# One set of three chain buffers, earlier loads of B11, and transposes spread among products, in a hybrid block on one core

## The chip, the core and the metric

The kernel runs on one core of one Trainium2 chip. The metric is device time in microseconds (us) of one execution. Engines: TensorE (PE; PEld is its weight load), VectorE (DVE), ScalarE (ACT), GpSimd (POOL) and SyncE (SP), which only issues loads here.

## The reference

A decoder block over 256 tokens of width 2048, all in float32: an mLSTM branch (4 heads of 256) and an attention branch (8 heads of 128), merged by sigmoid gates, a residual, and a squared-ReLU MLP of width 8192.

```python
    for l in range(DEPTH):
        xn = rmsnorm(x, norm_mix_pre[l])
        proj = jnp.einsum('bsd,dc->bsc', xn, w_in[l])
        mq, mk, mv, mo, mi, mf, aq, ak, av, g_m, g_a = split_cols(proj)
...
        h_m = (h * jax.nn.sigmoid(mo.astype(jnp.float32))).astype(dt)
...
        y_m = jnp.einsum('bsc,cd->bsd', h_m, w_branch_m[l])
        y_a = jnp.einsum('bsc,cd->bsd', h_a, w_branch_a[l])
        merged = jax.nn.sigmoid(g_m) * y_m + jax.nn.sigmoid(g_a) * y_a
        mix_out = jnp.einsum('bsd,de->bse', merged, w_out[l])
        x = x + rmsnorm(mix_out, norm_mix_post[l])

        hn = rmsnorm(x, norm_ffn_pre[l])
        u = jnp.square(jax.nn.relu(jnp.einsum('bsd,df->bsf', hn, w_up[l])))
        y = jnp.einsum('bsf,fd->bsd', u, w_down[l])
        x = x + rmsnorm(y, norm_ffn_post[l])
    return x
```

## The kernel before

Every weight comes from HBM once, in units of 1 MB (128 x 2048), and is split for TensorE into two parts: ScalarE casts the high half (`whi`, L175), VectorE subtracts it from the weight (`wlo`, L176). A product of two split operands is three matmuls (high by high, high by low, low by high), in `mm_tok` (L199), `mm_feat` (L194), `mm_feat_one` (L221) and `mm_factor` (L232, L236, L238). `whi` and `wlo` have four buffers each, two units.

The work is a list of steps; a step is a triple: load and split of its unit, its products, and what follows them (`post`). The loop at the end walks the list and emits the load and split of step i ahead of the products of step i-1. SP issues the loads in that order, and a load waits there until its buffer is free. Within that, a scheduler orders each engine's instructions.

The stages in order: projections (attention, mLSTM and output gate mo); gates and branches; the output product and the residual; the MLP.

**Gates.** The merge gates g_m and g_a are 4 column groups c. In group 0 the plain products are taken: `gate_steps(0, "m")` and `gate_steps(0, "a")`. Groups 1 to 3 go by `seven_steps(c)`: the two gates by two halves of the tokens make a 2 x 2 block product that seven products (p1, p2, p6, q3, q4, q5, q7) compute instead of eight, from sums of weight blocks. Each product has two steps u (two units of rows). Their left operands are x's (`xw`) and four prepared sums `fac`, which `open_gates` makes (ScalarE L678, VectorE L679) from tiles x that lie in `k8`. The weight sums build up in buffers: t starts as block B11 (a plain load on SP, L714, in `w_p1`), GpSimd adds a block to it by an accumulating load (L716) for q5, VectorE adds more for p6 and q4. z is a plain load (L706) and an accumulating load (L707) for q7. t lies in `k8`, a set of two buffers of 1 MB; z has a buffer of its own. `mixed` deals other steps among the seven: gates of group 0, then the branch products (`branch_steps`), whose `evac` multiplies by the gates. After group 3, `merged` transposes the sums (L797) and splits them into `mg` (L803).

**Residual.** `last_mix` computes the last column quarter of the output product for both halves h of the tokens; `residual(h)` makes the norm, adds to x in four pieces e (L886), transposes each (L891) and splits it into `hw`, pair by pair (ScalarE L896, VectorE L897). `hw` is the moving operand of the MLP's up products (L221 to L223). The splits of the first two up units are kept in places of their own (`first_places`).

**MLP.** Eight chunks of the width. For each but the last, `group(j, p)` takes the down product by the same seven-product scheme: `b12` (L1037) is loaded into `k8`, `bt` = B11 + b12 (L1038) is in `k8`, later + b22 (L1044), + b21 (L1060); b22 and b21 lie in `rawl`, two buffers. GpSimd accumulates into b12 (L1053). The operands `xs` come from `factors` (L970, L980 to L993) on ScalarE and VectorE. Up products of the next chunk (U) stand between the down steps (D).

Of the kernel before, what the change touches and what calls it, by code (L numbers as in the profile page):

```python
# [82 lines left out]
def tile_hybrid_block(ctx, tc, xT, xtok, pos, pre, small, wmix, wa, wi, wg, wbr, wo, wu, wd,  # L83
# [17 lines left out]
    def k8(name):  # L101
        return pk.tile([P, 2048], F32, name=name, tag="k8", bufs=2)
# [96 lines left out]
    def mm_tok(accs, parts, mov, kbase, start, stop, halves=(0, 1), n=512):  # L199

        for k, h in [(k, h) for k in range(4) for h in halves]:
# [489 lines left out]
    def gate_steps(c, n):  # L691

        for u in range(4):
            tok_step(wg["ma".index(n), c, u], ("g", n, c), xmov, u,
                     lambda h, acc: tanh(gate(n, c)[:, h], acc, h), bank=sm_tile)

    def seven_steps(c):
# [6 lines left out]
        def load_z(u):  # L704
            r["z", u] = pool["f"].tile([P, 2048], F32, name="z", tag="z", bufs=1)
# [81 lines left out]
    def merged(c):  # L787

        m = mg[c] = pool["f"].tile([P, 4, 2, T], F32R, name="mg", tag="fac", bufs=4)
        src = gt.pop(("m", c))  # L790
        del gt["a", c]
        for q in range(2):
            ps = sm_tile()
            for j in range(2):
                for h in range(2):
                    b = 2 * j + h
                    PE.transpose(out=ps[:, b * P:(b + 1) * P],  # L797
# [528 lines left out]
```

## Time and profile before

| | |
|---|---|
| median of 3 runs | 1507.71 us (1507.64 to 1510.67) |
| profiled execution | 1508.53 us, span 1506.7 us |
| TensorE busy | 1428.2 us (95%) |
| VectorE busy | 1182.1 us (78%) |
| ScalarE busy | 829.1 us (55%) |
| mean granted clock of TensorE | 0.975 of 2.4 GHz |
| loads | 297.28 MB, mean 197 GB/s |
| gates and branches | about 361 to 667 us of the span |
| residual | about 745 to 775 us |
| MLP | about 775 to 1500 us |

A matmul's busy time in the rows overlaps the next one's, so the pitch of products is read from starts. "Idle before" stands in brackets in a timeline, with what ended it.

### The profile page before, as it was taken

What the parts mean: (1) busy time and instruction counts of PE and PEld (TensorE: products, weight loads), DVE (VectorE), ACT (ScalarE), POOL (GpSimd) and SP (SyncE); (2) the same over time, 40 slices, a digit from 0 to 9 for tenths busy, and PEclk for the clock granted to TensorE, in tenths of its full rate; (3) what the DMA queues carried; (4) which work ended last, traced back from release to release, by engine and by line L of the source; (5) the groups of instructions that cost most, each with busy time, mean ns of one, the idle gap of its engine ahead of it and who ended that gap; (6) DMA issues with size and microseconds to landing.
All of it is one profiled execution on the core that took longest, in us unless ns stands there. A gap on an engine that the chain in (4) does not pass through costs nothing.

```text
span 1506.7 us, 20304 instructions
## 1 busy us (share of the span) xinstructions
PE 1428.2 (95%) x7892; PEld 1226.1 (81%) x7892; DVE 1182.1 (78%) x1506; ACT 829.1 (55%) x1132; POOL 24.7 (2%) x38
## 2 busy tenths in 40 slices
PE   8999999998798999999879999999999999999997
PEld 6888888886576877788679898989889798998985
DVE  7787766776576888854556989898999989889895
ACT  8655555555455556634555665555555555555562
POOL 0000000000000000000000000000000000000000
PEclk9999999998899999999989999999999999999999
DMA  7644444443669686655527476566575575665561
GB/s 229 223 166 173 168 168 168 168 168 140 197 189 271 206 285 202 231 220 183 221 84 252 168 236 203 180 222 215 203 242 199 176 250 177 215 226 194 196 223 57
DMA packets 46321, 297.28 MB, mean 197 GB/s; under 512 B 5392, under 2 KB 7568, under 8 KB 11664
## 3 DMA queue, kind: packets, MB, share of 16 engines
q1 hardware_dynamic: 42336, 268.71, 48.5%
q0 software_dynamic: 3744, 27.26, 9.5%
q8 instruction: 62, 1.02, 0.3%
q14 instruction: 35, 0.29, 0.1%
q10 hardware_dynamic: 144, 0.01, 0.0%
HBM read 293.86 MB, written 2.10 MB: 196 GB/s over the span
## 4 chain that ended last, share of the span: by engine, by line
PE 79%; DVE 11%; DMA 5%; ACT 2%; issue 2%; SPq 0%; DVEq 0%; ACTq 0%
PE acc L223 8%; PE acc L221 8%; PE acc L222 8%; PE acc L194 8%; PE acc L238 7%; PE acc L232 7%; PE acc L236 7%; DVE wlo L176 5%; PE acc L211 4%; PE acc L206 4%; PE acc L210 4%; PE acc L195 4%; PE sm L206 2%; PE sm L210 2%; PE sm L211 2%
## 5 line engine op out<-in xcount | busy, mean ns | idle before, releaser
L175 ACT CAST whi<-raw 128x1024 fp32r<-128x1024 f32 (+2 forms) x396 | 399.0, 1014 | 346.9 <-PE acc L222 109.3
L176 DVE TENSOR_TENSOR wlo<-raw,whi 128x1024 fp32r<-128x1024 f32 (+2 forms) x396 | 463.2, 1179 | 149.6 <-ACT whi L175 144.7
L223 PE MATMUL acc<-hw,wlo 128*128 128x256 f32 x992 | 284.5, 287 | 0.1
L222 PE MATMUL acc<-hw,whi 128*128 128x256 f32 x992 | 283.8, 286 | 0.0
L221 PE MATMUL acc<-hw,whi 128*128 128x256 f32 x992 | 283.1, 286 | 0.0
L223 PEld LDWEIGHTS acc<-hw,wlo 128*128 128x128 f32 x992 | 191.7, 193 | 4.3 <-DVE wlo L176 1.2
L221 PEld LDWEIGHTS acc<-hw,whi 128*128 128x128 f32 x992 | 191.0, 193 | 5.1
L222 PEld LDWEIGHTS acc<-hw,whi 128*128 128x128 f32 x992 | 191.1, 193 | 2.1
L232 PE MATMUL acc<-whi,xs 128*128 128x512 f32 x440 | 175.7, 400 | 17.4 <-ACT whi L175 17.4
L194 PE MATMUL acc<-xw,whi 128*128 128x512 f32 x512 | 183.5, 397 | 0.0
L238 PE MATMUL acc<-wlo,xs 128*128 128x512 f32 x440 | 174.0, 399 | 1.5 <-DVE wlo L176 1.2
L236 PE MATMUL acc<-whi,xs 128*128 128x512 f32 x440 | 174.7, 397 | 0.0
L195 PE MATMUL acc<-xw,wlo 128*128 128x256 f32 x512 | 146.5, 286 | 0.0
L175 ACT CAST whi<-bt 128x1024 fp32r<-128x1024 f32 x84 | 86.0, 1046 | 83.2 <-PE acc L222 40.6
L194 PEld LDWEIGHTS acc<-xw,whi 128*128 128x128 f32 x512 | 96.2, 188 | 22.9 <-issue 1.9
L176 DVE TENSOR_TENSOR wlo<-bt,whi 128x1024 fp32r<-128x1024 f32 x84 | 101.2, 1220 | 13.4 <-ACT whi L175 13.3
L232 PEld LDWEIGHTS acc<-whi,xs 128*128 128x128 f32 x440 | 83.2, 189 | 34.8 <-ACT whi L175 20.7
L238 PEld LDWEIGHTS acc<-wlo,xs 128*128 128x128 f32 x440 | 82.7, 188 | 22.1 <-DVE wlo L176 5.4
L236 PEld LDWEIGHTS acc<-whi,xs 128*128 128x128 f32 x440 | 83.3, 189 | 17.5
L195 PEld LDWEIGHTS acc<-xw,wlo 128*128 128x128 f32 x512 | 96.3, 188 | 1.3 <-issue 0.2
L175 ACT CAST whi<-rawl 128x1024 fp32r<-128x1024 f32 x56 | 58.6, 1047 | 47.5 <-PE acc L222 34.6
L176 DVE TENSOR_TENSOR wlo<-t,whi 128x1024 fp32r<-128x1024 f32 x48 | 57.7, 1222 | 33.9 <-ACT whi L175 32.1
(294 smaller groups left out, 2401.4 us busy)
## 6 DMA issues: line engine op xcount, KB each, us to landing
raw<-in_wu_dram SPq DMA_DIRECT2D x64, 1024.0 KB, 5.0
raw<-in_wi_dram SPq DMA_DIRECT2D x48, 1024.0 KB, 4.9
rawl<-in_wd_dram SPq DMA_DIRECT2D x28, 1024.0 KB, 4.9
raw<-in_wd_dram SPq DMA_DIRECT2D x22, 1024.0 KB, 5.8
raw<-in_wg_dram SPq DMA_DIRECT2D x20, 1024.0 KB, 5.1
raw<-in_wbr_dram SPq DMA_DIRECT2D x16, 1024.0 KB, 5.7
raw<-in_wo_dram SPq DMA_DIRECT2D x16, 1024.0 KB, 4.8
b<-in_wd_dram SPq DMA_DIRECT2D x14, 1024.0 KB, 5.3
```

What stands on the lines that cost most here:

```text
L175: S.copy(out=hi[:, s], in_=r)
L176: V.tensor_tensor(out=lo[:, s], in0=r, in1=hi[:, s].bitcast(F32), op=ALU.subtract)
L194: PE.matmul(out=accs[i][:, 0:2 * T], lhsT=hi, rhs=m, start=k == 0, stop=False)
L195: PE.matmul(out=accs[i][:, 0:T], lhsT=lo, rhs=m[:, 0, :], start=False, stop=k == nk - 1)
L206: first = PE.matmul(out=acc, lhsT=m[:, 0, ts], rhs=hi, start=start and k == 0, stop=False)
L210: PE.matmul(out=acc, lhsT=m[:, 1, ts], rhs=hi, start=False, stop=False)
L221: PE.matmul(out=acc, lhsT=hi, rhs=m[:, 0, :], start=k == 0, stop=False)
L222: PE.matmul(out=acc, lhsT=hi, rhs=m[:, 1, :], start=False, stop=False)
L223: PE.matmul(out=acc, lhsT=lo, rhs=m[:, 0, :], start=False, stop=k == KT - 1)
L232: first = PE.matmul(out=acc, lhsT=f[:, k, 0], rhs=hi, start=start and k == 0, stop=False, skip_group_check=more)
L236: PE.matmul(out=acc, lhsT=f[:, k, 1], rhs=hi, start=False, stop=False, skip_group_check=more)
L238: PE.matmul(out=acc, lhsT=f[:, k, 0], rhs=lo, start=False, stop=stop and k == 3, skip_group_check=more)
```

## The change

The set `k8` gets a third buffer, and takes t, z, b12, bt and b22 (before in `rawl`, which keeps one buffer), and both halves of the second up unit. A load of t is emitted by a hook (`before`) ahead of an earlier step: t of group 1 ahead of two steps of gate m(0), those of groups 2 and 3 ahead of p2(0) and p2(1) of the group before. z's first load follows p1(1) instead of p1(0). q5(1) comes right behind q7(0), and q3 accumulates into q5's bank. gate_steps(0, "m") uses the other kind of bank (`acc`), as does one of the two steps of branch m. The transposes of `merged` are spread over steps (`at`). `residual` is cut into `mix_rstd`, `add_mix`, `turn` and `operand`, dealt among the products of `last_mix`; the first two up units are split at earlier steps (`first_unit`). In the MLP v and u have buffers of their own, and all xs but q4's share one set (`g4`).

```diff
     def k8(name):
-        return pk.tile([P, 2048], F32, name=name, tag="k8", bufs=2)
+        return pk.tile([P, 2048], F32, name=name, tag="k8", bufs=3)
...
-    def gate_steps(c, n):
+    def gate_steps(c, n, bank=sm_tile):
...
+    ahead = {}
+    hooks = {}
+    def before(step, f, *args):
...
+        hooks.setdefault(id(step[1]), []).append(lambda: f(*args))
     def seven_steps(c):
...
         def load_z(u):
-            r["z", u] = pool["f"].tile([P, 2048], F32, name="z", tag="z", bufs=1)
+            r["z", u] = k8("z")
             nc.sync.dma_start(out=r["z", u], in_=w(1, 0, u))
             nc.gpsimd.dma_start(out=r["z", u], in_=w(1, 1, u), accum_op=ALU.add)
...
+        def load_t(u):
+            r["t", u] = k8("t")
+            nc.sync.dma_start(out=r["t", u], in_=w(0, 0, u))
         def w_p1(u):
-            t = r["t", u] = k8("t")
-            nc.sync.dma_start(out=t, in_=w(0, 0, u))
-            parts = split(t)
-            nc.gpsimd.dma_start(out=t, in_=w(1, 0, u), accum_op=ALU.add)
-            if u == 0:
+            parts = split(r["t", u])
+            nc.gpsimd.dma_start(out=r["t", u], in_=w(1, 0, u), accum_op=ALU.add)
+            if u == 1:
                 load_z(0)
             return parts
...
-        banks = dict(p1="a", p2="a", q5="e", q7="b", q4="b", p6="f", q3="g")
+        banks = dict(p1="a", p2="a", q5="e", q3="e", q7="b", q4="b", p6="f")
...
             elif name == "q3":
-                V.tensor_tensor(out=ga[:, 0], in0=ga[:, 1], in1=r["v"], op=ALU.subtract)
-                add(ga[:, 0], a)
+                V.tensor_tensor(out=ga[:, 0], in0=a, in1=r["v"], op=ALU.subtract)
...
-            more = name in ("p2", "q4")
+            more = name in ("p2", "q3", "q4")
...
+        ahead[c] = load_t
         return [step(n, u) for n, u in (
-            ("p1", 0), ("p1", 1), ("q5", 0), ("q7", 0), ("p6", 0), ("q3", 0), ("q5", 1),
+            ("p1", 0), ("p1", 1), ("q5", 0), ("q7", 0), ("q5", 1), ("p6", 0), ("q3", 0),
             ("p6", 1), ("q3", 1), ("q7", 1), ("p2", 0), ("q4", 0), ("p2", 1), ("q4", 1))]
...
         src = ha if n == "a" else hm
+        banks = [sm_tile, sm_tile] if n == "a" else [acc_tile, sm_tile]
...
-                     bank=sm_tile)
...
+                     bank=lambda: banks.pop()())
...
+    def merged(c, q):
+        if q == 0:
+            mg[c] = pool["f"].tile([P, 4, 2, T], F32R, name="mg", tag="fac", bufs=4)
+        m, src, ps = mg[c], gt["m", c], sm_tile()
+        for j in range(2):
...
-    gate_steps(0, "m")
+    def at(k, f, *args):
...
+        src, mm, post = steps[k]
+        steps[k] = src, mm, lambda: (post(), f(*args))
+    gate_steps(0, "m", acc_tile)
...
-    for k, f in ((i - 3, lambda: mlstm_out(3, heads.pop(3))), (i - 2, open_gates)):
...
-    both_gates(1, (gate_steps, 0, "a"))
-    both_gates(2, (branch_steps, 0, "a"), (branch_steps, 0, "m"), (branch_steps, 1, "a"))
-    both_gates(3, (branch_steps, 1, "m"), (branch_steps, 2, "a"), (branch_steps, 2, "m"))
-    then(lambda: [merged(c) for c in range(3)])
+    at(i - 3, lambda: mlstm_out(3, heads.pop(3)))
+    at(i - 2, open_gates)
+    groups = {c: seven_steps(c) for c in SGATES}
+    before(steps[i - 3], ahead[1], 0)
+    before(steps[i - 1], ahead[1], 1)
+    for c in (1, 2):
+        before(groups[c][10], ahead[c + 1], 0)
+        before(groups[c][12], ahead[c + 1], 1)
+    mixed(groups[1], (gate_steps, 0, "a"))
+    mixed(groups[2], (branch_steps, 0, "a"), (branch_steps, 0, "m"), (branch_steps, 1, "a"))
+    mixed(groups[3], (branch_steps, 1, "m"), (branch_steps, 2, "a"), (branch_steps, 2, "m"))
+    i = len(steps)
+    for k, c, q in ((9, 0, 0), (8, 0, 1), (5, 1, 0), (4, 1, 1)):
+        at(i - k, merged, c, q)
     branch_steps(3, "a")
     branch_steps(3, "m")
-    then(merged, 3)
+    for k, c, q in ((0, 2, 0), (1, 2, 1), (3, 3, 0), (3, 3, 1)):
+        at(i + k, merged, c, q)
...
-    def residual(h):
...
+    def mix_rstd(h):
...
+        late["r", h] = r
...
+    def add_mix(h, e):
+        x1 = late["x1"][:, h, e * 512:(e + 1) * 512]
+        pin(V.scalar_tensor_tensor(out=x1, in0=late["mix"][e][:, h], scalar=late["r", h], in1=x1,
+                                   op0=ALU.mult, op1=ALU.add))
+    def turn(h, e):
+        ps = late["ps", h, e] = sm_tile()
+        for j in range(4):
+            k = 4 * e + j
+            pin(PE.transpose(out=ps[:, j * P:(j + 1) * P],
+                             in_=late["x1"][:, h, k * P:(k + 1) * P], identity=ident))
...
+    def operand(h, e):
...
+            S.activation(out=hi, in_=p, func=AF.Copy, scale=g)
+            pin(V.scalar_tensor_tensor(out=lo, in0=p, scalar=g, in1=hi.bitcast(F32), op0=ALU.mult,
+                                       op1=ALU.subtract))
...
-                    mm_tok(late["acc"], units[i], mgmov, 8 + 4 * i, False, i == 1, halves=(h,))
+                    mm_tok(late["acc"], units[i], mgmov, 8 + 4 * i, False, i == 1, halves=(h,),
+                           after_k=turns if h and i else None)
                 if h == 0:
-                    residual(0)
+                    mix_rstd(0)
+                    for e in range(4):
+                        add_mix(0, e)
+        def turns(k):
+            if k > 0:
+                turn(0, k - 1)
+                operand(0, k - 1) if k < 3 else None
         def post():
-            keep_warm(8)
-            residual(1)
+            mix_rstd(1)
+            turn(0, 3)
+            keep_warm(12)
+            for e in range(4):
+                add_mix(1, e)
+                if e in (1, 2):
+                    operand(0, e + 1)
+                turn(1, e)
+                operand(1, e)
+            for h in range(2):
+                for e in range(4):
+                    square(late["x1"][:, h, e * 512:(e + 1) * 512], late["ss2"][:, h, e:e + 1])
             open_mlp()
         steps.append(([wo[14], wo[15]], mm, post))
+    def first_unit(i):
+        def place():
+            if i == 0:
+                a = pa.tile([P, 2, 2, 1024], F32R, name="wu0", tag="hm")
+                return [(a[:, h, 0], a[:, h, 1]) for h in range(2)]
+            b = [k8("wu1").bitcast(F32R) for _ in range(2)]
+            return [tuple(t[:, 1024 * h:1024 * h + 1024] for t in b) for h in range(2)]
+        places[len(steps)] = place
+        steps.append(([wu[i]], late.setdefault("first", []).extend, lambda: None))
...
     for e in range(4):
...
+            if (e, u) in ((2, 1), (2, 3)):
+                first_unit(u // 2)
     last_mix()
...
-        late["v"] = g4("v")
+        late["v"] = f.tile([P, 2, 512], F32, name="v")
...
-            uh[c] = g4("u", (4, T))
+            uh[c] = pool["f"].tile([P, 4, T], F32, name="u", tag="u", bufs=2)
...
-        if name[1] in ("p1", "q5", "p6"):
+        if name[1] != "q4":
             f = g4("xs", (4, 2, P)).bitcast(F32R)
         else:
-            f = pool["f"].tile([P, 4, 2, P], F32R, name="xs", tag="xs", bufs=4)
+            f = pool["f"].tile([P, 4, 2, P], F32R, name="xs", tag="xs", bufs=1)
...
-        return pool["f"].tile([P, 2048], F32, name="rawl", tag="rawl", bufs=2)
+        return pool["f"].tile([P, 2048], F32, name="rawl", tag="rawl", bufs=1)
...
         def w_t2():
-            r["22"] = long_raw()
+            r["22"] = k8("b22")
...
-    def first_places():
...
+    first = {}
+    def mm_first(units):
+        first["a"] = [acc_tile(), acc_tile()]
+        mm_feat_one(first["a"], late["first"], hmov, tail=4)
+    steps.append(([], mm_first, lambda: first_up(*first["a"])))
...
             src = steps[i][0]
+            for f in hooks.get(id(steps[i][1]), ()):
+                f()
```

Where rows move. First TensorE's queue at the end of gate m(0) and the start of group 1. Names: `mo`'s last products are L194/L195, gate products L206, L210, L211 (L207, L211, L212 in the new lines), `sm<-qkm` and `sm<-mv,ml_s` are the last mLSTM head's small products, `sm<-ident,t` its transposes. Before:

```order
L195 MATMUL acc<-xw,wlo 128x256
L538 MATMUL sm<-ident,t_3484 128x128 x2
L478 MATMUL sm<-rows,ident 128x384
L538 MATMUL sm<-ident,t_3486 128x128 x2
L488 MATMUL sm<-qkm 128x256 x2
L491 MATMUL sm<-qkm 128x128 x2
L499 MATMUL sm<-mv,ml_s 128x258
L503 MATMUL sm<-mv,ml_s 128x258
L505 MATMUL sm<-mv,ml_s 128x258
L206 MATMUL sm<-whi,xw 128x512
```

And now, at one of the places among the gate products, and, in the second fence, at their end:

```order
L491 MATMUL sm<-qkm 128x256
L494 MATMUL sm<-qkm 128x128 x2
L207 MATMUL acc<-whi,xw 128x512
L211 MATMUL acc<-whi,xw 128x512
L212 MATMUL acc<-wlo,xw 128x512
```

```order
L212 MATMUL acc<-wlo,xw 128x512
L235 MATMUL acc<-whi,xw 128x512
L239 MATMUL acc<-whi,xw 128x512
L241 MATMUL acc<-wlo,xw 128x512
...
L541 MATMUL sm<-ident,t_3679 128x128 x2
L541 MATMUL sm<-ident,t_3681 128x128 x2
L235 MATMUL acc<-whi,xw 128x512
```

The small products stood in a row ahead of the gate products and are now among them; p1(1,0) (L235, L239, L241, 12 products) follows the gate products, and the head's transposes, which lead to `fac`, stand between p1(1,0) and p1(1,1).

SP's queue of loads, from the start of the kernel to group 2. `wa`, `wi`, `wg` and `wbr` are the weights of the attention projections, of the others, of the gates and of the branches; p_i is the positions. Before:

```order
L158 DMA raw<-in_wa_dram 128x1040
L324 DMA p_i<-in_pos_dram 128x256
L158 DMA raw<-in_wa_dram 128x1040 x7
L158 DMA raw<-in_wi_dram 128x2048 x48
L158 DMA raw<-in_wg_dram 128x2048 x7
L706 DMA z<-in_wg_dram 128x2048
L714 DMA t<-in_wg_dram 128x2048 x2
L158 DMA raw<-in_wg_dram 128x2048
L706 DMA z<-in_wg_dram 128x2048
L158 DMA raw<-in_wg_dram 128x2048 x4
L706 DMA z<-in_wg_dram 128x2048
L158 DMA raw<-in_wbr_dram 128x2048
```

And now:

```order
L724 DMA t<-in_wg_dram 128x2048
L327 DMA p_i<-in_pos_dram 128x256
L158 DMA raw<-in_wa_dram 128x1040 x7
L158 DMA raw<-in_wi_dram 128x2048 x48
L158 DMA raw<-in_wg_dram 128x2048 x7
L724 DMA t<-in_wg_dram 128x2048
L716 DMA z<-in_wg_dram 128x2048
L158 DMA raw<-in_wg_dram 128x2048
L716 DMA z<-in_wg_dram 128x2048
L158 DMA raw<-in_wg_dram 128x2048 x4
L724 DMA t<-in_wg_dram 128x2048
L158 DMA raw<-in_wbr_dram 128x2048
```

The first t stands ahead of p_i, the second ahead of z; group 2's first t stands where its z stood, and that z five rows later.

VectorE's queue at the third chunk start of the MLP. Before:

```order
L1079 TENSOR_TENSOR y_6293<-y_6293,acc_9314 128x512
L970 TENSOR_TENSOR xs_9303<-u_9005,xs_9303 128x4x128
L985 TENSOR_TENSOR s_b_9298<-s_a_9293,u_8618 128x512
...
L970 TENSOR_TENSOR xs_9300<-s_b_9298,xs_9300 128x4x128
L1038 TENSOR_TENSOR bt_9409<-raw_9358,b12_9408 128x2048
L176 TENSOR_TENSOR wlo_9387<-raw_9384,whi_9386 128x1024
```

And now:

```order
L1129 TENSOR_TENSOR y_6291<-y_6291,acc_9312 128x512
L1088 TENSOR_TENSOR bt_9407<-raw_9356,b12_9406 128x2048
L1035 TENSOR_TENSOR s_b_9296<-s_a_9291,u_8616 128x512
...
L1020 TENSOR_TENSOR xs_9298<-s_b_9296,xs_9298 128x4x128
L1020 TENSOR_TENSOR xs_9301<-u_9003,xs_9301 128x4x128
```

The sum bt stands nine rows earlier, right behind y, and an operand xs later.

## Rows read from the trace of the kernel before

**Rows 1.** The page: busy times, and the chain that ended last by engine.

```profile
PE 1428.2 (95%) x7892; PEld 1226.1 (81%) x7892; DVE 1182.1 (78%) x1506; ACT 829.1 (55%) x1132; POOL 24.7 (2%) x38
PE 79%; DVE 11%; DMA 5%; ACT 2%; issue 2%; SPq 0%; DVEq 0%; ACTq 0%
```

**Rows 2.** TensorE's waits by releaser: us in total, times, longest.

```profile
PE acc L232 <- ACT whi L175: 29.3, 12, 7.0
PE sm L891 <- DVE x L886: 12.9, 4, 3.9
...
PE sm L797 <- DVE mg L803: 3.2, 1, 3.2
```

**Rows 3.** Window of groups 1 and 2: busy times, clock, DMA share, GB/s.

```profile
403.00:550.00 147.00, 137.35 (x546) 105.98 (x547) 114.70 (x99) 82.33 (x87) 6.81 (x8) 0.95 0.78 232
```

**Rows 4.** Windows at half clock: PE, PEld, DVE, ACT, POOL busy; clock; DMA share; GB/s.

```profile
363.48:373.71 10.23, 5.92 (x15) 4.70 (x16) 3.26 (x10) 1.76 (x4) 0.00 (x0) 0.50 0.24 94
401.02:407.85 6.83, 4.81 (x11) 3.35 (x12) 2.36 (x2) 1.99 (x2) 0.86 (x1) 0.50 1.03 272
482.94:489.77 6.83, 6.31 (x16) 4.86 (x16) 5.20 (x5) 3.46 (x5) 0.84 (x1) 0.50 0.82 146
...
1093.93:1097.35 3.42, 3.04 (x12) 2.85 (x13) 3.42 (x6) 1.41 (x3) 0.84 (x1) 0.50 0.87 271
```

**Rows 5.** The chain in order of time: start, us, what.

```profile
24.41 3.46 DMA raw<-in_wa_dram
...
393.32 4.64 DVE fac L679 x4
397.98 10.61 DMA t<-in_wg_dram
...
409.74 1.24 DVE wlo L176
...
431.51 11.05 DMA raw<-in_wg_dram
...
469.41 11.69 DMA t<-in_wg_dram
```

**Rows 6.** TensorE's timeline at the gates: start, us, instructions, idle before.

```profile
362.62 0.67 PE L488 MATMUL sm<-qkm 128*128 128x256 f32 x2 [1.57 <-DVE ml_e L483]
...
372.25 0.99 PE L206 MATMUL sm<-whi,xw 128*128 128x512 f32 x1
...
391.46 0.38 PE L538 MATMUL sm<-ident,t 128*128 128x128 f32 x2
...
391.92 0.39 PE L210 MATMUL sm<-whi,xw 128*128 128x512 f32 x1
...
395.63 0.40 PE L211 MATMUL sm<-wlo,xw 128*128 128x512 f32 x1
403.00 0.80 PE L232 MATMUL acc<-whi,xw 128*128 128x512 f32 x1 [6.97 <-ACT whi L175]
...
482.30 0.50 PE L232 MATMUL acc<-whi,xw 128*128 128x512 f32 x1 [3.46 <-ACT whi L175]
```

**Rows 7.** DMA issues: count, KB each, median us from issue to landing.

```profile
raw<-in_wu_dram SPq DMA_DIRECT2D x64, 1024.0 KB, 5.0
...
z<-in_wg_dram POOLq DMA_DIRECT2D x6, 1024.0 KB, 11.9
```

**Rows 8.** The chain at the residual's end.

```profile
752.14 0.36 DVE hw L897
...
752.93 0.36 DVE hw L897
...
773.63 1.22 PE acc L221 x4
```

**Rows 9.** MLP: TensorE's waits, 905 to 1450; VectorE's timeline; a window.

```profile
PE acc L232 <- ACT whi L175: 16.9, 7, 2.8
...
1090.82 2.28 DVE L1038 TENSOR_TENSOR bt<-raw,b 128x2048 f32<-128x2048 f32 x1
...
1090.00:1100.00 10.00, 7.17 (x40) 6.17 (x39) 10.00 (x12) 4.17 (x5) 0.84 (x1) 0.83 0.55 142
```

More of the change, by code (lines that the diff above doesn't have):

```diff
@@ L197, in mm_feat, with mm_tok @@
                 after_k(k)
-    def mm_tok(accs, parts, mov, kbase, start, stop, halves=(0, 1), n=512):
+    def mm_tok(accs, parts, mov, kbase, start, stop, halves=(0, 1), n=512,
+               after_k=None):
         for k, h in [(k, h) for k in range(4) for h in halves]:
@@ L211, in mm_tok @@
             PE.matmul(out=acc, lhsT=m[:, 0, ts], rhs=lo, start=False, stop=stop and k == 3)
+            if after_k:
+                after_k(k)
     def mm_feat_one(accs, units, mov, after_k=None, tail=0):
@@ L689, in tanh @@
         S.activation(out=out, in_=src, func=AF.Tanh, scale=rhalf[:, h:h + 1])
-    def gate_steps(c, n):
+    def gate_steps(c, n, bank=sm_tile):
         for u in range(4):
             tok_step(wg["ma".index(n), c, u], ("g", n, c), xmov, u,
-                     lambda h, acc: tanh(gate(n, c)[:, h], acc, h), bank=sm_tile)
+                     lambda h, acc: tanh(gate(n, c)[:, h], acc, h), bank=bank)
+    ahead = {}
+    hooks = {}
+    def before(step, f, *args):
+        hooks.setdefault(id(step[1]), []).append(lambda: f(*args))
     def seven_steps(c):
@@ L784, in branch_steps @@
             tok_step(wbr["am".index(n), c, u], ("b", n, c), lambda k: src[:, k], u, evac, last=1,
-                     bank=sm_tile)
[L787 to L797, printed above, removed]
-                                 in_=src[:, h, (2 * q + j) * P:(2 * q + j + 1) * P],
-                                 identity=ident)
-            hi, lo = (m[:, 2 * q:2 * q + 2, i] for i in range(2))
-            p = ps.rearrange("p (k t) -> p k t", t=T)
-            S.activation(out=hi, in_=p, func=AF.Copy, scale=0.5)
-            V.scalar_tensor_tensor(out=lo, in0=p, scalar=0.5, in1=hi.bitcast(F32), op0=ALU.mult,
-                                   op1=ALU.subtract)
+                     bank=lambda: banks.pop()())
[5 more added lines that the diff above has]
+            for h in range(2):
+                b = 2 * j + h
+                PE.transpose(out=ps[:, b * P:(b + 1) * P],
+                             in_=src[:, h, (2 * q + j) * P:(2 * q + j + 1) * P], identity=ident)
+        hi, lo = (m[:, 2 * q:2 * q + 2, i] for i in range(2))
+        p = ps.rearrange("p (k t) -> p k t", t=T)
+        S.activation(out=hi, in_=p, func=AF.Copy, scale=0.5)
+        V.scalar_tensor_tensor(out=lo, in0=p, scalar=0.5, in1=hi.bitcast(F32), op0=ALU.mult,
+                               op1=ALU.subtract)
     def mixed(first, *parts):
@@ L1182, in down_group @@
         return [(part(n, 0), part(n, 1), part(n, 2)) for n in range(7)]
-    def first_places():
-        a = pa.tile([P, 2, 2, 1024], F32R, name="wu0", tag="hm")
-        b = [k8("wu1").bitcast(F32R),
-             pool["f"].tile([P, 2048], F32, name="wu1", tag="z", bufs=1).bitcast(F32R)]
-        return [[(a[:, h, 0], a[:, h, 1]) for h in range(2)],
-                [tuple(t[:, 1024 * h:1024 * h + 1024] for t in b) for h in range(2)]]
-    feat_step([wu[0], wu[1]], hmov, first_up, tail=4, product=mm_feat_one)
-    places[len(steps) - 1] = first_places
+    first = {}
[3 more added lines that the diff above has]
+    steps.append(([], mm_first, lambda: first_up(*first["a"])))
     for i in range(2, 8):
```

38 lines of the change are left out of this document (7 added, 31 removed).

## The prediction

> **What bounds the kernel now.** The page's busy times come first: TensorE works 95% of the span, VectorE 78%, and the chain that ended last runs through TensorE for 79% [rows 1]. So the end moves only where TensorE waits, or where its products run at half clock after a wait. The waits by releaser say where: casts that feed products of L232 cost 29.3 us in 12 waits, four transposes of the residual 12.9 us, one transpose of merged 3.2 us [rows 2]. The window of gate groups 1 and 2 gives the DMA engines' share, 0.78 [rows 3], so loads there compete. The windows with the granted clock show the second price: after each long wait the clock stands at 0.50, that is 1.2 of 2.4 GHz, for 3.42 to 10.23 us [rows 4]. The chain in order of time names what was late: twice a t load, once a raw load [rows 5]. TensorE's timeline has the waits one by one, and gives a product's pitch: 16 steps from 391.92 to 395.63, so 0.232 us [rows 6]. The own time is 1508.53 us, 1.83 over its span and 0.8 over the median of 1507.71; the sum is made against 1508.53.
>
> **The change part by part.**
>
> *Start of the kernel.* t(1,0) now goes out right behind the first loads, ahead of p_i and seven raw loads. The chain still runs through a load at 24.41 us [rows 5], so a megabyte in front can push what follows by its own length, some 4 us. But the next casts on VectorE don't use what is pushed: they stand ahead of the rotary work that needs p_i. I take 0, bounds -1 and +4.
>
> *The last mLSTM head and gate m(0).* Before, TensorE stops at 361.05, waits 1.57 us, begins the head's last small products at 362.62 and the gate products at 372.25 [rows 6]: 11.2 us, most of them at half clock and with TensorE busy 5.92 of 10.23 us [rows 4], and the first three gate products take 0.8 us more by that clock. Now these products stand among the 96 gate products, which need only raw loads and x. The small ones still cost about 1.2 us (14 of 128 to 384 columns, against 0.232 for 512). The gain is 11.2 + 0.8 - 1.2, some 10.5 us: the last gate product ends at 385.4 instead of 395.9.
>
> *t loads of group 1.* p1(1,0) needs t(1,0), which before was issued behind the third of the fac operations on VectorE (four take 4.64 us from 393.32), so that TensorE waited 6.97 us at 403.00; and p1(1,1) began only when its own t, issued at 397.98, had landed 10.61 us later and ScalarE had cast it, at 409.74, where VectorE's cast begins [rows 5, 6]. Now t(1,0) is there: its 12 products follow the gate ones at once, 2.8 us, to 388.2. t(1,1) is still not early: two of the three k8 slots hold the x tiles that fac reads. The transposes that lead to fac stand behind p1(1,0); before, from these transposes (391.46) to the third fac operation's end it was 5.4 us. So t(1,1) is issued near 393.7. With nothing but z beside it I take 6 us to land (5.0 is a load's median [rows 7], 10.61 the crowded case) and 1.1 for the cast: p1(1,1) starts at 400.8, 9 us before 409.74. The 10.5 us are thus not added to this; much of the idle time moves to a wait of 12 us between p1(1,0) and p1(1,1), with a half-clock stretch behind it as before [rows 4]. Bounds -5 (load of 10.6) and -11.
>
> *The rest of group 1.* A raw load of 11.05 us stands in the chain at 431.51 [rows 5]; with t and z not bunched behind fac it should be shorter. I take -2, bounds 0 and -4.
>
> *Groups 2 and 3.* t(2,0) and t(2,1) are issued ahead of p2(0) and p2(1) of the group before. So the load of 11.69 us at 469.41 goes from the chain, and with it the wait of 3.46 us at 482.30, 0.5 us behind it, and half of the 6.31 us that TensorE was busy at half clock: -7. Group 3 had no such wait at its start. But z now takes the third slot of the same set, which t of the group before holds until q4(1) has been cast: z(2,0) and z(3,0) come later. z needs a plain load and an accumulating load of 11.9 us in the median [rows 7], 18 us with the cast. Ahead of q7(0) stand 36 products of its group and 24 of another step, 14 us, and the slot is freed one step (24 products) before the group's start: 19 to 20 us against 18, and with busy DMA engines 1 us of wait each, +2, bounds 0 and +14 (7 each with the clock).
> The bytes of the stage are the same in less time. At 232 GB/s for 147 us [rows 3] groups 1 and 2 move 34 MB; at 272 GB/s, the most in [rows 4], that is 125 us, so a gain of 17 is not excluded, but loads take longer: +2, bounds 0 and +6.
>
> The Trainium skill, page "DMA: Bandwidth & Descriptors", section "Issuing engines are not separate DMA queues", says that transfers started from any engine run on the same 16 DMA engines and interleave. By that rule an earlier t load is paid for by whatever it runs beside; the trace agrees (10.61 us for t beside another t and z, against a median of 5.0). If all of it were paid at the start, the sum below would be 4 us higher; that is the second of the rivals.
>
> *Turns of merged.* The transposes that stood in one row after group 3 are spread over it, so the wait of 3.2 us for mg [rows 2] goes: -3, bounds 0 and -4. Branch m's second bank (acc) and the q5/q3 bank shared (three VectorE subtractions of 0.7 us fewer, one a group) are off the path: VectorE is busy 114.70 of 147 us there [rows 3]. 0.
>
> *Residual.* h1's 24 products (5.6 us) now cover part of half 0's chain, and its turns stand among them; the four waits were 12.9 us [rows 2]. Against that, VectorE's order puts three casts of the up weights (1.24 us each, as at 409.74 [rows 5]) into the chain for half 0, so a new wait at the first turn is 4 to 5 us. The up products begin near 767.3 instead of 773.63 [rows 8], but then meet operands that are made in pairs (ScalarE, then VectorE), one per 0.79 us from 752.14 to 752.93 [rows 8], 16 for half 1: they give back most of 6.3 us. I take -2.5, bounds -7 and +3.
>
> *MLP, six chunk starts.* The waits for the cast of bt are 16.9 us [rows 9], 2.76 each, and 3.42 us at half clock follow each [rows 4], 1.6 lost: 4.4 each, 26 in all. bt's add (2.28 us) moves nine rows up in VectorE's queue, as b12 has a slot. But VectorE is then busy 10.00 of 10.00 us [rows 9]: what is put ahead of other casts makes these late. Following the products through the new order, stalls of some 0.4 to 1.7 us stand at four or five places ahead of the old one. I take -0.8 each, -5, bounds 0 and -26.
>
> Sum: 0 - 9 - 2 - 7 + 2 + 2 - 3 - 2.5 - 5 = -24.5, so 1508.5 - 24.5 = **1484 us**. In the gate stage -17, in the rest -7.5.
>
> **The rivals.**
> *z becomes the late load.* If the accumulating load runs as slow as t's 10.61 plus 11.9, q7(0) of groups 2 and 3 waits 5 us each and half clock takes 2: +12 instead of +2, 1494. For it: DMA share 0.8; against it: t no longer runs beside it.
> *The first t load is paid at the start.* +4: 1488. For it: the chain runs through loads until 28 us; against it: the casts stand ahead of p_i's work.
> *The change doesn't do what it says:* t(1,1) and z(1,0) land where they did, since fac frees the slots, and everything waits there; the first term falls from -9 to 0: 1493. For it, fac's chain has ScalarE and VectorE steps of other heads ahead; against it, TensorE reaches the transposes some 3 us earlier.
> *The chunk starts are cleared.* VectorE's debt is made good elsewhere, -26 instead of -5: 1463. Against it: 10.00 of 10.
> *Slower.* SP issues in order. z of groups 2 and 3 waits on SP for q4(1)'s slot, and wbr and wg loads stand behind it in the queue. If they land after their products want them, each group pays their landing time. It decides from 12 us a group on (24.5 over two groups); with a load of 10 us behind z's and another behind it, 17 each, 34 in all: 1518. Against it: raw has buffers loaded ahead.
>
> **How the numbers follow.** Forecast 0.48 (own range 1476 to 1491), z late 0.15, start 0.10, no earlier landing 0.10, chunk starts cleared 0.09, slower 0.08. 1465 to 1503 leaves out the slower case and most of the cleared one, 0.17. A measurement of this kernel tells 0.2% (3 us) from no change. Faster takes in all but the slower rival and a tail of the late z: 0.89; same 0.04; slower 0.07.
>
> **What would show it.** Right: gate products follow the mo products with no wait; a wait of 9 to 13 us on L232's successor (L235) at p1(1,1), which begins at 399 to 402; group 2 begins without a wait for t; group 3 begins 15 to 20 us earlier than at 557; small waits at the chunk starts, with new ones ahead. Wrong: waits on casts of z over 3 us, rows of raw that land late behind z, a wait of more than 6 us at turn(0,0), or VectorE with free time at the chunk starts.

## The result, and the profile after

The changed kernel takes 1491.51 us (median of 4 runs, 1489.58 to 1492.45) against 1508.6 us for the kernel before on the same chip: ratio 0.9883, 95% interval 0.9866 to 0.9900. It is 17 us faster where 24.5 were forecast; 1491.5 lies in the range of 1465 to 1503. It also lies just outside the range that the prediction gave to its own mechanism (1476 to 1491), and closer to three rivals (1488, 1493 and 1494) than to 1484, so the time alone does not say which mechanism held; the traces below do.

The page after, to be held against [rows 1], with the DMA queues (packets, MB, share of 16 engines; q1 are SP's loads, q0 GpSimd's):

```profile
PE 1419.9 (95%) x7900; PEld 1216.1 (82%) x7900; DVE 1178.7 (79%) x1503; ACT 830.3 (56%) x1133; POOL 24.7 (2%) x38
...
q1 hardware_dynamic: 42336, 268.71, 48.9%
q0 software_dynamic: 3744, 27.26, 9.7%
```

GpSimd's 27 MB of accumulating loads take 0.36% of the DMA engines' span for each MB, SP's 269 MB 0.18%. That factor of two is not in the prediction, though the page before had it already:

```profile
q1 hardware_dynamic: 42336, 268.71, 48.5%
q0 software_dynamic: 3744, 27.26, 9.5%
```

Most of what the prediction missed hangs on these loads (experiments 3 and 4).

The stages are best compared by the start of the same product in both traces: for the gates by its place in the order, behind them by its number counted from the end. The difference is after minus before, worked out from the two timelines, so from one execution of each kernel:

| product | before | after | difference |
|---|---|---|---|
| first gate m(0) product | 372.25 | 361.16 | -11.1 (of it +1.8 from the start of the kernel) |
| last gate m(0) product | 395.63 | 387.28 | -8.4 |
| p1(1,1) | 409.76 | 402.11 | -7.7 |
| a product near the end of group 1 (p2, q4) | 472.14 | 466.79 | -5.4 |
| third product of group 2's q5 | 494.85 | 480.73 | -14.1 |
| end of group 2 | 554.84 | 544.83 | -10.0 |
| 108 products on, in group 3 | 580.85 | 578.00 | -2.9 |
| first product of the output matrix | 660.75 | 652.75 | -8.0 |
| second up unit of the MLP | 804.65 | 795.43 | -9.2 |
| last product | 1496.98 | 1479.60 | -17.4 |

TensorE's timeline after (start, us, instruction, idle before and what ended it) shows why the gates lose again what they had won:

```profile
361.16 0.39 PE L207 MATMUL acc<-whi,xw 128*128 128x512 f32 x1
...
387.28 0.40 PE L212 MATMUL acc<-wlo,xw 128*128 128x512 f32 x1
...
402.11 0.79 PE L235 MATMUL acc<-whi,xw 128*128 128x512 f32 x1 [11.20 <-ACT whi L175]
...
421.85 0.50 PE L235 MATMUL acc<-whi,fac 128*128 128x512 f32 x1 [4.29 <-ACT whi L175]
...
485.40 0.50 PE L235 MATMUL acc<-whi,fac 128*128 128x512 f32 x1 [2.18 <-ACT whi L175]
...
563.32 0.79 PE L235 MATMUL acc<-whi,fac 128*128 128x512 f32 x1 [4.85 <-ACT whi L175]
```

The first three rows answer to [rows 6] and are as forecast: gate products from 361, a wait of 11.2 us at p1(1,1), which begins at 402.11. The last three are waits that were not there before: for t(1,1) at q5(1) of group 1, for z(2,0) at q7(0) of group 2, and for t(3,0) at q5(0) of group 3. The chain after shows their loads:

```profile
405.61 15.05 DMA t<-in_wg_dram
...
470.70 13.51 DMA z<-in_wg_dram
...
542.01 4.86 DMA z<-in_wg_dram
...
547.46 0.51 POOL z L717
547.96 14.18 DMA t<-in_wg_dram
```

The loads of 15.05, 13.51 and 14.18 us are accumulating ones, issued by GpSimd; the one of 4.86 us is z(3,0)'s plain load, whose end z's accumulating load waits for. GpSimd's timeline shows how they came together; group 3 before:

```profile
534.88 0.84 POOL L707 DMA_DIRECT2D z<-in_wg_dram  x1 [31.46 <-DVE t L710]
557.41 0.86 POOL L716 DMA_DIRECT2D t<-in_wg_dram  x1 [21.69 <-DVE wlo L176]
562.61 0.84 POOL L716 DMA_DIRECT2D t<-in_wg_dram  x1 [4.34 <-DVE wlo L176]
```

and after:

```profile
547.43 0.84 POOL L717 DMA_DIRECT2D z<-in_wg_dram  x1 [52.96 <-DVE wlo L176]
547.96 1.19 POOL L728 DMA_DIRECT2D t<-in_wg_dram  x1
550.27 0.84 POOL L728 DMA_DIRECT2D t<-in_wg_dram  x1 [1.11 <-DVE wlo L176]
```

Before, z's went out 22 us ahead of t's, into its own buffer. Now z waits for the slot that t of the group before leaves (z(3,0)'s plain load goes out at 542.01, before at 529.27, while the group itself begins 10 us earlier), and all three go out within 3 us. They land one after another, 7.78, 14.18 and 17.90 us after their issue, at 555.21, 562.14 and 568.17. In group 2 it is much the same, and in group 1 two of them meet, z(1,0)'s and t(1,1)'s. So z is not the load that got slower, as the medians from issue to landing show, before (z's is 11.9, [rows 7]) and after:

```profile
t<-in_wg_dram POOLq DMA_DIRECT2D x6, 1024.0 KB, 8.6
```

```profile
t<-in_wg_dram POOLq DMA_DIRECT2D x6, 1024.0 KB, 14.6
...
z<-in_wg_dram POOLq DMA_DIRECT2D x6, 1024.0 KB, 7.9
```

Windows over the three late loads (last columns: granted clock, DMA share, GB/s):

```profile
547.96:562.14 14.18, 10.51 (x46) 8.19 (x44) 4.38 (x5) 3.41 (x5) 2.04 (x3) 1.00 0.98 220
470.70:484.20 13.50, 12.52 (x54) 9.80 (x52) 8.66 (x7) 4.88 (x6) 1.70 (x2) 1.00 1.02 227
405.61:420.65 15.04, 11.83 (x50) 8.92 (x48) 8.12 (x6) 4.02 (x5) 1.19 (x2) 1.00 0.95 226
```

The DMA engines are full at 220 to 227 GB/s. The prediction took 272 GB/s as what the stage could still move. That the shared slot brings the loads together is read from these timelines; no run gives z a buffer of its own beside the set of three.

### The profile page after: what moved, and what is told of

It is laid out like the page before. It is cut to its first block, busy times and chain, and to the rows that moved or that the text cites. A ratio compares the mean times of both kernels' runs of the same rounds, so it can differ in the third digit from the quotient of the medians.

```text
span 1489.3 us, 20301 instructions
## 1 busy us (share of the span) xinstructions
PE 1419.9 (95%) x7900; PEld 1216.1 (82%) x7900; DVE 1178.7 (79%) x1503; ACT 830.3 (56%) x1133; POOL 24.7 (2%) x38
## 3 DMA queue, kind: packets, MB, share of 16 engines
q8 instruction: 62, 1.02, 0.3%
## 4 chain that ended last, share of the span: by engine, by line
PE 80%; DVE 10%; DMA 5%; ACT 2%; issue 1%; SPq 0%; POOL 0%; DVEq 0%; ACTq 0%; POOLq 0%
PE acc L194 8%; PE acc L241 8%; PE acc L235 8%; PE acc L239 8%; PE acc L226 7%; PE acc L225 7%; PE acc L224 7%; PE acc L212 5%; PE acc L207 5%; PE acc L211 5%; DVE wlo L176 5%; PE acc L195 4%; DMA t<-in_wg_dram 2%; DMA z<-in_wg_dram 2%; PE sm L207 2%; PE sm L211 2%
## 5 line engine op out<-in xcount | busy, mean ns | idle before, releaser
L226 PE MATMUL acc<-hw,wlo 128*128 128x256 f32 x992 | 280.3, 283 | 1.8 <-DVE wlo L176 1.5
L225 PE MATMUL acc<-hw,whi 128*128 128x256 f32 x992 | 279.4, 282 | 0.0
L224 PE MATMUL acc<-hw,whi 128*128 128x256 f32 x992 | 277.5, 283 | 0.3 <-ACT whi L175 0.3
L226 PEld LDWEIGHTS acc<-hw,wlo 128*128 128x128 f32 x992 | 187.1, 189 | 8.4 <-DVE wlo L176 6.5
L224 PEld LDWEIGHTS acc<-hw,whi 128*128 128x128 f32 x992 | 185.7, 188 | 6.2 <-ACT whi L175 2.7
L225 PEld LDWEIGHTS acc<-hw,whi 128*128 128x128 f32 x992 | 187.0, 188 | 1.6
L241 PE MATMUL acc<-wlo,xs 128*128 128x512 f32 x440 | 174.4, 400 | 10.3 <-DVE wlo L176 10.0
L194 PE MATMUL acc<-xw,whi 128*128 128x512 f32 x512 | 183.6, 397 | 0.0
L235 PE MATMUL acc<-whi,xs 128*128 128x512 f32 x440 | 174.5, 396 | 3.8 <-ACT whi L175 3.1
L239 PE MATMUL acc<-whi,xs 128*128 128x512 f32 x440 | 173.3, 394 | 0.0
L195 PE MATMUL acc<-xw,wlo 128*128 128x256 f32 x512 | 146.4, 286 | 0.0
L194 PEld LDWEIGHTS acc<-xw,whi 128*128 128x128 f32 x512 | 96.2, 188 | 23.1 <-issue 2.1
L241 PEld LDWEIGHTS acc<-wlo,xs 128*128 128x128 f32 x440 | 82.7, 188 | 36.5 <-DVE wlo L176 20.3
L235 PEld LDWEIGHTS acc<-whi,xs 128*128 128x128 f32 x440 | 82.7, 188 | 20.2 <-ACT whi L175 4.9
L207 PE MATMUL acc<-whi,xw 128*128 128x512 f32 (+1 forms) x256 | 95.2, 375 | 2.8 <-ACT whi L175 2.8
L195 PEld LDWEIGHTS acc<-xw,wlo 128*128 128x128 f32 x512 | 96.3, 188 | 1.1
L239 PEld LDWEIGHTS acc<-whi,xs 128*128 128x128 f32 x440 | 82.6, 188 | 17.2
L211 PE MATMUL acc<-whi,xw 128*128 128x512 f32 (+1 forms) x256 | 94.9, 374 | 1.1 <-DVE xw L255 1.1
```

The lines of the kernel that those rows point to most:

```text
L194: PE.matmul(out=accs[i][:, 0:2 * T], lhsT=hi, rhs=m, start=k == 0, stop=False)
L195: PE.matmul(out=accs[i][:, 0:T], lhsT=lo, rhs=m[:, 0, :], start=False, stop=k == nk - 1)
L207: first = PE.matmul(out=acc, lhsT=m[:, 0, ts], rhs=hi, start=start and k == 0, stop=False)
L211: PE.matmul(out=acc, lhsT=m[:, 1, ts], rhs=hi, start=False, stop=False)
L224: PE.matmul(out=acc, lhsT=hi, rhs=m[:, 0, :], start=k == 0, stop=False)
L225: PE.matmul(out=acc, lhsT=hi, rhs=m[:, 1, :], start=False, stop=False)
```

## The experiments

Ratios are to runs of the kernel before beside them on the same chip, with 95% intervals; the changed kernel's is 0.9883 (0.9866 to 0.9900).

**1. t's loads at their written place.**

```diff
-            nc.sync.dma_start(out=r["t", u], in_=w(0, 0, u))
+            tc.keep_in_program_order(nc.sync.dma_start(out=r["t", u], in_=w(0, 0, u)))
```

> The changed kernel, but the six plain loads of t keep their written place in SP's queue, so t(1,0) no longer goes out ahead of p_i at the start. My theory: the early load costs the 1.8 us that the first mLSTM products come later than before, and nothing else hangs on it; so -1 to -2.5 us against the changed kernel, with the last mo product back near 359.4 us instead of 361.2, and p1(1,0) still without a wait behind the gate products. Rival: t(1,0) then lands too late behind the raw loads of gate m(0), p1(1,0) waits 2 us or more, and the gain is used up: within 1 us.

0.9877 (0.9862 to 0.9893). In the trace the first 300 us run 1.2 us earlier than in the changed kernel: in the chain p_i lands after 4.45 us instead of 7.84. p1(1,0) has no wait. The direction is as expected; the gain is too small to show in the ratio. The traces of all these kernels bear it out: the 1861st product of TensorE, near the end of the mo products, starts at 355.76 to 356.42 us in the four traces with t's loads at their written place (experiments 1, 10, 11, 12; 355.87 before the change), and at 356.78 to 358.92 in the nine with the early load.

**2. GpSimd's order t, t, z.**

```diff
-            nc.gpsimd.dma_start(out=r["z", u], in_=w(1, 1, u), accum_op=ALU.add)
+            tc.keep_in_program_order(
+                nc.gpsimd.dma_start(out=r["z", u], in_=w(1, 1, u), accum_op=ALU.add))
...
-            nc.gpsimd.dma_start(out=r["t", u], in_=w(1, 0, u), accum_op=ALU.add)
+            tc.keep_in_program_order(
+                nc.gpsimd.dma_start(out=r["t", u], in_=w(1, 0, u), accum_op=ALU.add))
```

> The changed kernel, but GpSimd issues both accumulating loads of t ahead of those of z in each group, as the code writes them (the scheduler had put z between or ahead). My theory: what groups 1 and 3 wait for (4.29 us at 421.85, 4.85 us at 563.32) is t's accumulating load held behind z's and sharing the DMA engines with it (15.05 and 14.18 us to landing); with t first these take 8 to 10 us, both waits go, and with the half clock behind them -6 to -11 us. Rival: z, which now goes out last, is late for q7(0) instead, and a wait of 3 to 8 us for it takes the place in each group: within 3 us.

0.9969 (0.9953 to 0.9985): 13 us slower than the changed kernel, worse than either expected. Its chain and TensorE's timeline in group 3:

```profile
559.93 18.38 DMA z<-in_wg_dram
...
579.51 0.79 PE L235 MATMUL acc<-whi,fac 128*128 128x512 f32 x1 [9.12 <-ACT whi L175]
```

t's loads land in time, and z, the last to go out, takes 18.38 us in group 3 and is awaited by q7: waits of 4.74, 8.14 and 9.12 us in the three groups. So the order does not make the loads cheaper; it chooses who waits, and how long, by how soon the last one is wanted.

**3. Without z's second block** (q7's right operand is one block instead of a sum of two).

```diff
-            nc.gpsimd.dma_start(out=r["z", u], in_=w(1, 1, u), accum_op=ALU.add)
```

> The changed kernel without z's accumulating loads: q7 then uses one weight block instead of a sum of two, so 6 MB are left out. My theory (accumulating loads in flight together are the late ones): the three waits at 421.85, 485.40 and 563.32 (11.3 us) fall below 1 us each, and with the clock -11 to -17 us. Rival (a slot of the set of three or SP's queue holds t and z up, or the stage's bytes as a whole): the waits stay over 2 us each, and the gain is under 5 us.

0.9779 (0.9761 to 0.9797), 15.7 us less than the changed kernel (the difference of the ratios times 1508.6, here and below). The kernel leaves out 6 MB of loads. TensorE's waits for casts from 400 to 640 us:

```profile
PE acc L235 <- ACT whi L175: 11.2, 1, 11.2
```

Of the waits for ScalarE's casts only the one at p1(1,1) is left, and no wait for VectorE's casts is over 0.74 us. A late slot or SP's queue does not make the waits by itself, since neither is touched by this edit; the 6 MB fewer are not ruled out as the cause until the next experiment.

**4. z's second block by a plain load and VectorE.**

```diff
-            nc.gpsimd.dma_start(out=r["z", u], in_=w(1, 1, u), accum_op=ALU.add)
+            V.tensor_tensor(out=r["z", u], in0=r["z", u], in1=load(w(1, 1, u)), op=ALU.add)
```

> The changed kernel, but z's second block comes by a plain load into one of the three raw buffers and VectorE adds it (2.28 us each, 6 times), in place of GpSimd's accumulating load. My theory: the waits come from accumulating loads lying together, of which two are left, 8 and 13 us; the plain load takes some 5. So the three waits go as without the second block (-15.7 us by the ratios), less what the raw buffers lose: -6 to -14 us. Rival: it is SP's queue and the raw buffers that bound the stage, then the added raw loads make other products wait: no gain, or some us slower.

0.9820 (0.9805 to 0.9835), 9.5 us less. The same bytes come in, so it is the way they come, and not their number, that cost these 9.5 us; the sum takes VectorE 2.29 us each time. Waits of 1.69 and 2.99 us for t(c,0)'s accumulating load are left in groups 2 and 3.

**5. GpSimd's order t, z, t.** load_z(0) stands ahead of t(c,1)'s accumulating load in w_p1, and both are held in that order as in 2.

> The changed kernel with GpSimd's order held at t(c,0), z(c,0), t(c,1) in all three groups, the order in which the products want them; by the trace only group 3's differs (z, t, t). My theory: group 3's wait of 4.85 us goes, since t(3,0) no longer waits behind z(3,0) whose plain load lands 6 us later; -3 to -7 us. Rival: z(3,0) then becomes late for q7 by as much: within 2 us.

0.9859 (0.9842 to 0.9876): some 3.6 us less, but the intervals overlap, so it is not told apart from the changed kernel or from the rival. Group 3's wait is 2.21 instead of 4.85 us, and it is now for z (14.41 us to landing): part of what t no longer waits, z does.

**6. The old place of q5(1).**

```diff
-            ("p1", 0), ("p1", 1), ("q5", 0), ("q7", 0), ("q5", 1), ("p6", 0), ("q3", 0),
+            ("p1", 0), ("p1", 1), ("q5", 0), ("q7", 0), ("p6", 0), ("q3", 0), ("q5", 1),
```

> The changed kernel with the old place of q5(1) (behind q3(0)) and q3's own bank and second VectorE operation. My theory: the three accumulating loads of a group share the DMA engines and take 8, then 13 to 15, then 17 us when they go out together; the change made their last user, q5(1), come three products earlier. So group 1's wait of 4.29 us for t(1,1) goes; group 3's order on GpSimd becomes t, z, t too, so its 4.85 us fall; group 2's 2.18 us stay: -4 to -9 us. Rival: the third load is late for q7 or p6 in any order (as with t first, 14 us slower): within 3 us.

0.9864 (0.9831 to 0.9898): not told apart from the changed kernel. The waits change their places: none at 421.85, 2.44 us at 440.00 for q5(1,1)'s operand, 2.42 in group 3.

**7. The MLP's old sets for u, v and xs.**

```diff
-        if name[1] != "q4":
+        if name[1] in ("p1", "q5", "p6"):
...
-            uh[c] = pool["f"].tile([P, 4, T], F32, name="u", tag="u", bufs=2)
+            uh[c] = g4("u", (4, T))
```

v goes back to g4 in the same way, and the other xs to a set of four buffers.

> The changed kernel with the MLP's u, v and xs in the sets of before (u and v share the set g4 with xs of p1, q5 and p6), but b12, bt and b22 still in the set of three. By the trace at equal products the MLP gave 8.3 us. My theory: what moved bt up is the third buffer, which lets b12 land before the boundary; so the own buffers matter little and it is within 2 us. Rival: the sets for u and xs let VectorE take the operands later, and without them the waits of 2.76 us at the chunk starts come back: +5 to +9 us.

0.9868 (0.9848 to 0.9888): not told apart. TensorE's waits from 905 to 1450 us in this kernel (us in total, times, longest):

```profile
PE acc L241 <- DVE wlo L176: 9.6, 11, 1.3
PE acc L235 <- ACT whi L175: 5.1, 11, 0.8
```

and in the changed kernel:

```profile
PE acc L241 <- DVE wlo L176: 9.5, 16, 1.3
PE acc L235 <- ACT whi L175: 2.8, 7, 1.2
```

In neither is there a wait of 2.76 us as in [rows 9]. Own buffers for u and v are not what removed it. What is left of the MLP's change is the set of three, with b22 in it; that this is the cause is argued by elimination, and no run takes it away alone.

**8. The residual of before** in the changed kernel (residual(h) in one piece, the first two up units split at their old place).

> The changed kernel with the residual of before: transposes behind each piece's sum, squares in each half, the first two up units split at their old place. By the trace at equal products the residual's part gave 1.1 us, so +0.5 to +3 us against the changed kernel, with four waits for the turns near 13 us in all again. Rival: the residual's part is worth as much as the waits it removes (12.9 us before, some 6 now) and another stage gives it back: +5 to +8 us.

0.9880 (0.9863 to 0.9898): not told apart. The waits for the turns are back, and what they cost in the end is less than these intervals, some 2.6 us either way, can tell:

```profile
PE sm L908 <- DVE x L903: 13.2, 4, 3.9
```

**9. Two gate a(0) steps between p1(1,0) and p1(1,1).**

```diff
-    mixed(groups[1], (gate_steps, 0, "a"))
+    i = len(steps)
+    mixed(groups[1], (gate_steps, 0, "a"))
+    moved = [s for s in steps[i:] if s not in groups[1]][:2]
+    steps[i:] = groups[1][:1] + moved + [s for s in steps[i + 1:] if s not in moved]
```

> The changed kernel with two of the four steps of gate a(0) (48 products, 11.2 us) put between p1(1,0) and p1(1,1), where TensorE now waits 11.20 us for t(1,1). My theory: this wait is only moved work's price and its products fill it; they are then missing later in group 1, where t(1,1)'s and z's accumulating loads are awaited, so part comes back: -3 to -9 us. Rival: what is awaited in group 1 in the end is z and t(1,1) after fac, whatever stands before, so that the wait only moves to q7 and q5: within 2 us.

0.9871 (0.9848 to 0.9894): the rival. The wait is shorter, but p1(1,1) begins later, at 410.60 instead of 402.11:

```profile
410.60 0.79 PE L235 MATMUL acc<-whi,xw 128*128 128x512 f32 x1 [4.42 <-ACT whi L175]
421.86 0.79 PE L235 MATMUL acc<-whi,fac 128*128 128x512 f32 x1 [3.62 <-ACT whi L175]
```

In this order the head's transposes come among the filling products, so fac begins on VectorE at 401.09 instead of 392.64, and frees t's slot that much later. Near the end of group 1 this trace is 0.8 us ahead of the changed kernel's (465.96 against 466.79), and in group 3 its three accumulating loads go out within 1.1 us, the wait there is 8.35 us, and it falls 3 us behind.

**10. Experiments 4 and 1 together; 11. these with 9 and with a branch step of groups 2 and 3 moved behind p1(1).**

> z's second block added by VectorE (ratio 0.982 alone) and t's plain loads kept in their written place in SP's queue (1.2 us less at the start in its trace). My theory: the two don't touch: ratio about 0.981. Rival: t(1,0) behind raw loads makes the crowded stage later: 0.982 or above.

> All together: z's second block by VectorE, t's loads in their written place, two gate a(0) steps between p1(1,0) and p1(1,1), and in groups 2 and 3 the branch step that stood between p1(0) and p1(1) put behind p1(1), so that t's accumulating load has 5.6 us more before q5(0) (waits of 1.69 and 2.99 us in the kernel with VectorE's sum). My theory: -3 to -8 us for the filled wait, -4 to -6 for the two others: 1470 to 1478 us against 1509 of before, ratio 0.974 to 0.980. Rival: each filler is missing elsewhere, and it stays at 0.981.

0.9812 (0.9796 to 0.9828), and 0.9850 (0.9830 to 0.9870). The first is as expected. The second misses its range and is slower than its parts without the fillers: the waits for t(c,0) stay, 2.71 and 2.87 us, and p1(1,1) begins at 407.96. Why t(c,0)'s load doesn't land earlier beside its users was not followed up, so the cause of this loss stays open.

**12. t(c,0)'s block by VectorE too**, on top of 10.

```diff
-            nc.gpsimd.dma_start(out=r["t", u], in_=w(1, 0, u), accum_op=ALU.add)
+            if u == 0:
+                add(r["t", u], load(w(1, 0, u)))
+            else:
+                nc.gpsimd.dma_start(out=r["t", u], in_=w(1, 0, u), accum_op=ALU.add)
```

> The kernel with z's second block added by VectorE and t's loads in their written place (ratio 0.981), and t(c,0)'s block for q5(0) too comes by a plain load and a VectorE addition, so that one accumulating load a group is left, t(c,1)'s. My theory: the two waits left in groups 2 and 3, 2.19 and 3.59 us for t(c,0)'s accumulating load of 8 us, go: ratio 0.976 to 0.979. Rival: the raw loads now stand in SP's queue behind three raw buffers, and their users wait instead: 0.981 or above.

0.9800 (0.9787 to 0.9814), 1481.31 us: the fastest of all that compute the whole result, 29 us under the kernel before (1510.68 in these runs). It lies between the two expectations, and the gain over 10 is within the intervals. Group 2's wait is down to 0.5 us; group 3 keeps one, now for t(3,1):

```profile
560.74 0.50 PE L235 MATMUL acc<-whi,fac 128*128 128x512 f32 x1 [2.62 <-ACT whi L175]
```

This load was the only accumulating one in flight and still took 13.28 us, beside five plain ones, with the DMA engines full:

```profile
546.26:559.54 13.28, 11.86 (x50) 9.02 (x49) 11.01 (x9) 5.63 (x6) 0.84 (x1) 1.00 1.01 297
```

So it is not only other accumulating loads that make one late, but full DMA engines, which accumulating loads fill sooner.

## Why the prediction was right, and where it was off

By its own steps (forecast, then measured from the table, in us; each measured value is from one trace of each kernel):

- *Start of the kernel*: 0; +1.8. The load in front was paid, but by 1.2 to 1.8 us and not by its whole 4 us (experiment 1); the step that the casts on VectorE hide all of it was wrong. The rule cited from the Trainium skill ("DMA: Bandwidth & Descriptors", "Issuing engines are not separate DMA queues") told the direction. The trace of experiment 1 agrees with it: without the load in front p_i takes 4.45 us to land, with it 7.84.
- *Last mLSTM head and t loads of group 1*: -9; -9.5 (-7.7 less the 1.8). Right in place and size: the gate products' end, the slot freed by fac (t(1,1) was issued at 396.16 and landed in 4.82 us), the wait of 11 us that stays. (Its sum 11.2 + 0.8 - 1.2 is 10.8 and not 10.5; measured is some 10 without the start. Nothing rests on it.) Experiment 9 shows that this wait is tied to fac's chain.
- *Rest of group 1*: -2; +2.3. Group 2's start: -7; -8.7. Right for group 2's start: its t loads left the chain.
- *z's later slot* (+2) *and the stage's bytes* (+2): measured +4.1 in group 2 and +7.1 in the first products of group 3, with the half clock behind each wait. Together with group 1, these terms were put at +2 and came to +13.5; that is all of the miss and more. In two other kernels that are the same there (experiments 7 and 8) the +7.1 is +6.4 and +9.6. The failed step is that z alone was given a price, 5 for its plain load and 11.9 for its accumulating one: t's own accumulating loads, which now go out beside z's, have no term in the sum. They are what got slower, from 8.6 to 14.6 us in the median, while z's fell to 7.9. The check by bytes, that at 272 GB/s a gain of 17 is not excluded, hid this, since an accumulating load takes the DMA engines twice as long for each byte: they were full at 220 to 227 GB/s. Of those in flight together the first lands after some 8 us, the second after 12 to 15 and the third after 17 to 20, whoever is first (experiments 2, 3, 5, 9). The rival "z becomes the late load" gave a sum that fits better (1494, against 1491.5 measured) and named the place in group 2, q7, but its mechanism holds there alone; in groups 1 and 3 it was t that was late. Of the signs set out beforehand, group 3 begins 10 us earlier, not 15 to 20, and no wait for z is over 3 us: the sign looked at the wrong load.
- *Turns of merged and the rest of group 3*: -3; -5.2 (from -2.9 to -8.0).
- *Residual*: -2.5; -1.2, and by experiment 8 not told from 0. The timeline has a wait at the first turn of 4.08 us, as forecast, and then waits for the pairs of hw, of which keep-warm products cover some:

```profile
746.06 0.66 PE L908 MATMUL sm<-ident,x 128*128 128x128 f32 x4 [4.08 <-DVE x L901]
752.22 0.66 PE L908 MATMUL sm<-ident,x 128*128 128x128 f32 x4 [1.64 <-DVE hw L919]
756.34 4.90 PE L150 MATMUL sm<-ones 128*128 128x128 f32 x24 [3.46 <-DVE hw L919]
762.41 0.51 PE L224 MATMUL acc<-hw,wu 128*128 128x256 f32 x2 [0.46 <-ACT hw L918]
```

The up products begin 11.2 us earlier than the 773.63 of [rows 8], 3.2 more than the stage had at its start, and two of these are gone by the second up unit.
- *MLP*: -5; -8.2. A chunk takes 89.04 us from one of these waits to the next, before 90.4 (from 1094.31 to 1184.67). The long wait and the half clock behind it are gone, and short waits for VectorE's casts stand in their place (timeline, and a window over one chunk with the granted clock 1.00):

```profile
1076.94 0.50 PE L241 MATMUL acc<-wlo,xs 128*128 128x512 f32 x1 [0.74 <-DVE wlo L176]
...
1078.68 0.50 PE L241 MATMUL acc<-wlo,xs 128*128 128x512 f32 x1 [0.53 <-DVE wlo L176]
...
1076.94:1165.98 89.04, 87.03 (x552) 76.95 (x552) 82.26 (x84) 51.37 (x60) 1.70 (x2) 1.00 0.63 212
```

The mechanism (VectorE full, stalls moved ahead) was right. The term was mis-sized by 0.5 us a chunk: the granted clock stays at 1.00 over the whole chunk, where before 3.42 us at half clock followed the long wait.

The sum was thus right in sign and in the mechanism of its gains, with the accumulating loads far too cheap. That it came within 7 us is in part luck: a miss of 11.5 us on those loads was offset by 3.2 us more from the MLP, and by smaller sums, that were not forecast. The gains themselves are read from the traces: of the parts that bring them, only the residual and the MLP's own buffers were taken back in a run (experiments 7 and 8), and neither showed.

## What to carry to other kernels

Before a load is moved, list all loads that will be in flight beside it, by their DMA time and not by their bytes, and by who needs them first; a transfer that was early by its own buffer goes out later when the buffer is shared, and then makes others late (read from the timelines, not tested alone). Where VectorE has room, a plain load and an addition may be cheaper than an accumulating load (here 9.5 us for six of them). A wait that hangs on a chain of casts is not filled by other steps' products if these delay the same chain (experiment 9).

## What the runs showed of the hardware

An accumulating load of 1 MB with no other load in flight (t(1,0) in the changed kernel, issued at 383.24) took 9.0 us to land, the first of several 7.7 to 8.4, a plain one with few beside it 4.8 to 5.0. For each byte it takes twice the DMA time of a plain one (0.36 against 0.18% of the span per MB). With several in flight the DMA engines were full (share 0.95 to 1.02) at 220 to 227 GB/s; with plain loads alone, in the second window, they moved more:

```profile
383.24:392.25 9.01, 7.67 (x36) 6.02 (x34) 4.31 (x20) 4.89 (x12) 1.00 (x1) 1.00 0.65 118
640.00:650.00 10.00, 10.00 (x47) 8.15 (x46) 5.46 (x7) 3.73 (x5) 0.00 (x0) 1.00 0.95 388
```

Short waits of TensorE (0.74 and 0.53 us at the chunk starts) left the granted clock at 1.00; the wait of 4.85 us in group 3 was followed by 0.50, as was the one of 2.76 us before ([rows 4]):

```profile
563.32:567.00 3.68, 3.64 (x8) 2.44 (x9) 3.68 (x4) 3.53 (x4) 0.00 (x0) 0.50 1.03 211
```
